# A Fourier and Hyena encoder layer: the first batch's loads and norm rearranged, one token's split done once, products of high parts before those of low parts

## The chip, the cores and the metric

The kernel runs on one core of a Trainium2 chip. Five engines with their own instruction queues work beside each other: TensorE (PE: matmuls, with its weight loads shown apart as PEld), VectorE (DVE), ScalarE (ACT), GpSimd (POOL) and SyncE (SP), which here only issues DMAs. The metric is the device time of the whole program in microseconds.

## What is computed

Two sequences of 1024 tokens and 1024 channels go through one encoder layer in float32. Cut to what matters:

```python
xn = rmsnorm(x, g_pre)
p = xn @ w_in
fv, fg, hv, hg, mg = split(p)                    # 1024, 1024, 3072, 1024, 2048 columns
fz = real(fftn(fv.reshape(B, L, 4, 256), axes=(1, 3), norm="ortho"))
y_f = (fz * silu(fg)) @ w_fourier_out
v, x1, x2 = split(short_conv(hv, w_short))       # width 3 over the sequence
kf = hyena_filters(...)      # small sine network: h = sin(f1*(z@w1+b1)); h = sin(f2*(h@w2+b2)); ...
z = v
for n, gate in enumerate((x1, x2)):
    z = gate * long_conv(z, kf[:, n], hyena_d[n])    # circular convolution of length 2048
y_h = (z * silu(hg)) @ w_hyena_out
g_f, g_h = split(sigmoid(mg + b_merge))
return x + rmsnorm((g_f * y_f + g_h * y_h) @ w_out, g_post)
```

## The kernel before

Every large product is made of three: each float32 operand is split into a high part `h` (rounded to the matmul format `fp32r`) and a low part `l` (the rest), and `mm3` adds `h*h`, `h*l` and `l*h` in one PSUM bank. `split` does it: ScalarE rounds (L171, the rows named CAST), then VectorE or GpSimd subtracts (L181). `mm` (L194) is the line of nearly all matmuls, so in the profile they are told apart by tile names, not by lines.

A planner orders the instructions. The code is traced in program order; the framework simulates a timeline, picks on each engine what is ready with the earlier place in the program first, and writes fixed orders with semaphores. An instruction can move far ahead of its place if its buffer is free. `issue_after(ins)` forces the instructions that a block puts on `ins`'s engine behind `ins`; `keep_in_program_order` pins one. Tiles with the same tag share a given number of buffers.

The stages, in order of time:

- `phase_fourier`, to about 230 us, for batch b = 0 and 1. `hidden(0)` computes the first layer of the sine network: two products (`phd`), a range reduction on VectorE (`sin_of`), two sines on ScalarE with the table that sines need, and a store to `d_h1`. `norm` loads eight row tiles `x` of 128 tokens, squares each on ScalarE with the sum of the row (`ss`), computes the reciprocal root for four rows at a time with three Newton steps in small VectorE instructions (`rstd`, tiles `rs_m`, `rs_t`, `rs`) and scales the identity by it (`dg`). `xtile` then multiplies rows by `dg` for each channel tile k = 0..7, which normalises and transposes at once (`tpx`, two PSUM banks of tag "T", four products of 128 tokens each), copies it out with the gain on ScalarE (`xg`, two buffers, 0.5 MB each), stores it (`d_x`), forms sums and differences of mirrored tokens (`eo`; in batch 1 the difference is made by GpSimd) and splits them (`eh`, `el`). Token 512 has no mirror and is kept apart in `x5`. `weights` loads a tile of `w_fv` (`wfv`), folds it (`wer`, `wor`) and splits it (`we`, `wo`). `pfv` multiplies. In batch 0 and the first half of the channels, six of the eight PSUM results grow while k runs (`begun`: four of the even part, two of the odd part); `fourier_half` makes the other two, splits all eight (`ee`, `oo`), multiplies `x5` (`pfx`), and runs the transforms over tokens with the table `seq` (`pse`, `pso`) and over channels with `chan` (`pP`, `pQ`). Batch 1 and the other halves follow.
- `phase_main`, to about 1700 us: input projections (`inproj`, PSUM `pin`, 1472 products of each of the three kinds), the filters' spectra (`pft`, `pXf`), and the two long convolutions by blocked transforms (`forward`: `pX`; `conv_back`: `pT`). In `inproj` GpSimd makes the low part of the weights (`wl`).
- `phase_gates` (`pg`) and `phase_out` (`pyf`, `pyh` from `project`, `po` from `last_rows`), with a block scheme that takes seven products instead of eight; its products come from `times`.

The tables `seq` (2 MB) and `chan` are loaded by GpSimd's queue, since they change their type on the way. So that they do not start too early, GpSimd first copies one element of `rs`, known only when the norm is done, into them (L531). `alt`, `chx` and `vec` have no such condition.

The lines the prediction touches: 237 to 254 `rstd`, 271 the sines, 317 the row loads, 320 the squares, 325 `dg`, 338 the clearing of two spare columns of `xg`, 344 and 345 the copy to `xg` and its store, 364 the weight load, 173 and 181 the split of `x5`, 531 to 535 the tables, 739 to 742 the weights of `inproj`.

## Time and profile before

| | |
|---|---|
| median of 3 runs | 2446.82 us (2443.44 to 2447.43) |
| profiled execution | 2449.26 us, span of its trace 2447.1 us |
| granted TensorE clock, mean | 0.997 of full speed |
| TensorE busy | 2396.1 us, 13196 matmuls |
| VectorE, ScalarE, GpSimd busy | 1893.8, 1096.8, 485.9 us |
| moved by DMA | 429.36 MB, mean 175 GB/s |

A row of the profile names the line, the engine, the operation and the tiles (`out<-in`), then the shapes, the number of instructions, their busy time and mean length, the idle time of the engine just before them and what ended it. `pin<-xl,wh` is thus a projection with the low part of x and the high part of the weight. Matmuls are pipelined and overlap in the records: those of 512 columns are shown as about 390 ns long and start about 227 ns apart. Small groups are counted by records; a float32 product that is not split shows two. The chain follows the work that ended last backwards to what released each step.

### The profile page before, as it was taken

The numbers are of one execution on the slowest core, as the hardware profiler recorded it, in microseconds if no ns is written. First come the engines' busy times: TensorE is split into PE (matmuls) and PEld (weight loads), VectorE is DVE, ScalarE is ACT, GpSimd is POOL, SyncE is SP. The second block draws the span as 40 slices with busy tenths as digits, with TensorE's granted clock in tenths as the row PEclk, the third lists the DMA queues.
The fourth block names the chain that finished last, engine by engine and source line by source line (L and its number), as shares of the span: only waits on it lengthen the run. The fifth ranks groups of instructions, "written<-read, shape, count | busy, mean of one in ns | idle before, by whom it ended". The sixth has DMA issues, their size and how long they took to land.

```text
span 2447.1 us, 36853 instructions
## 1 busy us (share of the span) xinstructions
PE 2396.1 (98%) x13196; PEld 2082.3 (85%) x13196; DVE 1893.8 (77%) x3405; ACT 1096.8 (45%) x2063; POOL 485.9 (20%) x516
## 2 busy tenths in 40 slices
PE   6999999999999999999999999999999999999998
PEld 5988888888888888888888888888788888888886
DVE  7687888888748999999989999766555455665677
ACT  5545677767633433334223333333344444544343
POOL 1341222222143433331000000112200111122111
PEclk9999999999999999999999999999999999999999
DMA  7545655555555555445434444335454567776543
GB/s 273 170 141 191 224 175 173 167 175 167 173 194 177 172 177 173 165 165 192 146 128 134 141 141 138 121 121 184 154 174 159 198 210 255 245 250 213 169 164 129
DMA packets 225151, 429.36 MB, mean 175 GB/s; under 512 B 23542, under 2 KB 87255, under 8 KB 224456
## 3 DMA queue, kind: packets, MB, share of 16 engines
q1 hardware_dynamic: 198444, 333.34, 41.1%
q0 software_dynamic: 26336, 93.65, 10.9%
q8 instruction: 104, 1.70, 0.3%
q14 instruction: 79, 0.65, 0.1%
q10 hardware_dynamic: 188, 0.02, 0.0%
HBM read 290.60 MB, written 136.31 MB: 174 GB/s over the span
## 4 chain that ended last, share of the span: by engine, by line
PE 88%; DMA 5%; issue 3%; DVE 2%; ACT 1%; POOL 1%; SPq 0%; DVEq 0%; POOLq 0%; ACTq 0%
PE pin L194 41%; PE pT L194 7%; PE pg L194 7%; PE pX L194 7%; PE po L194 6%; PE pyh L194 5%; PE pyf L194 5%; PE pXf L194 3%; PE pfv L194 2%; DMA wr<-in_w_fo 1%; PE pft L194 1%; PE tph L792 1%; DMA wr<-in_w_ho 1%; PE tpx L194 1%; DMA wfv<-in_w_fv 1%
## 5 line engine op out<-in xcount | busy, mean ns | idle before, releaser
L194 PE MATMUL pin<-xh,wl 128*128 128x512 f32 x1472 | 577.2, 392 | 2.6 <-POOL wl L181 2.6
L194 PE MATMUL pin<-xl,wh 128*128 128x512 f32 x1472 | 575.6, 391 | 2.4 <-DVE xl L181 2.4
L194 PE MATMUL pin<-xh,wh 128*128 128x512 f32 x1472 | 576.5, 392 | 0.7 <-DMA wh<-d_w 0.7
L181 POOL TENSOR_TENSOR wl<-wr,wh 128x512 fp32r<-128x512 f32 x136 | 240.3, 1768 | 1144.0 <-ACT wh L171 1105.9
L194 PEld LDWEIGHTS pin<-xh,wl 128*128 128x128 f32 x1472 | 277.1, 188 | 54.9 <-POOL wl L181 4.1
L194 PEld LDWEIGHTS pin<-xl,wh 128*128 128x128 f32 x1472 | 277.1, 188 | 54.3 <-DVE xl L181 3.2
L194 PEld LDWEIGHTS pin<-xh,wh 128*128 128x128 f32 x1472 | 277.1, 188 | 52.1 <-DMA wh<-d_w 1.1
L171 ACT CAST wh<-wr 128x512 fp32r<-128x512 f32 x264 | 162.8, 619 | 346.0 <-PE pin L194 136.8
L194 PE MATMUL pT<-cinv,yh 128*128 128x256 f32 x1024 | 193.1, 283 | 0.0
L194 PEld LDWEIGHTS pT<-cinv,yh 128*128 128x128 f32 x1024 | 164.0, 190 | 9.0
L181 DVE TENSOR_TENSOR t<-pX,k 128x1024 f32<-128x1024 f32 x128 | 155.9, 1218 | 10.9 <-PE pX L194 9.3
L194 PE MATMUL pX<-bh,cfwd 128*128 128x256 f32 x768 | 159.6, 286 | 0.0
L181 DVE TENSOR_TENSOR wl<-wr,wh 128x512 fp32r<-128x512 f32 x128 | 87.2, 687 | 93.5 <-ACT wh L171 93.2
L194 PE MATMUL pyf<-sf,wh 128*128 128x512 f32 x512 | 158.0, 390 | 0.9 <-ACT wh L171 0.9
L194 PE MATMUL pyh<-sh,wh 128*128 128x512 f32 x512 | 157.3, 389 | 0.0
L171 ACT CAST bh<-b 128x512 fp32r<-128x512 f32 x144 | 89.0, 620 | 126.7 <-DVE b L181 84.5
L194 PE MATMUL pT<-cinv,yl 128*128 128x256 f32 x512 | 144.9, 283 | 0.0
L171 ACT CAST yh<-y 128x512 fp32r<-128x512 f32 x128 | 79.2, 619 | 114.1 <-DVE y L181 91.3
L194 PEld LDWEIGHTS pX<-bh,cfwd 128*128 128x128 f32 x768 | 126.3, 190 | 2.5
L194 PEld LDWEIGHTS pyf<-sf,wh 128*128 128x128 f32 x512 | 96.0, 188 | 21.3 <-ACT wh L171 1.6
L194 PEld LDWEIGHTS pyh<-sh,wh 128*128 128x128 f32 x512 | 96.1, 188 | 19.9
L194 PE MATMUL pX<-bl,cfwd 128*128 128x256 f32 x384 | 109.6, 285 | 0.0
(354 smaller groups left out, 5262.7 us busy)
## 6 DMA issues: line engine op xcount, KB each, us to landing
k<-d_k SPq DMA_DIRECT2D x128, 512.0 KB, 4.0
wr<-in_w_in SPq DMA_DIRECT2D x136, 256.0 KB, 3.1
d_g<-gt SPq DMA_DIRECT2D x124, 256.0 KB, 2.6
d_k<-kt SPq DMA_DIRECT2D x128, 128.0 KB, 2.1
d_k<-kt SPq DMA_DIRECT2D x64, 256.0 KB, 2.3
wr<-in_w_fo POOLq DMA_DIRECT2D x64, 256.0 KB, 4.0
g<-d_g SPq DMA_DIRECT2D x64, 256.0 KB, 4.2
wr<-in_w_ho POOLq DMA_DIRECT2D x64, 256.0 KB, 3.7
```

The costliest lines, as they stand in the source:

```text
L171: self.rounded = nc.scalar.copy(h, src)
L181: return e.tensor_tensor(out, a, b, op=op)
L194: return self.nc.tensor.matmul(out, lhsT, rhs, start=start, stop=stop, skip_group_check=shared)
L792: nc.tensor.transpose(tp[:, q * P:(q + 1) * P], eo[:, e, q], self.ident)
```

## The change

- Row loads of batch 0 are issued by SP (even rows) and by ScalarE's queue (odd rows), all before the first square; the load of the first weight tile comes between rows 4 and 6 on SP's queue.
- The norm of batch 0 runs in three groups of rows, 0 to 3, 4 to 6 and 7. The first weight tile is folded before the last group and split behind the last scaling; all other weights' VectorE instructions in that loop are placed behind the last scaling too.
- The two sines of `hidden(0)` and the store behind them come after the last square.
- The tables are asked for when k = 4, and `seq` and `chan` wait for one element of tile 4 (`xg`).
- Token 512 is copied per tile into `r5` by ScalarE and split once after the loop, in both batches.
- In batch 0 the last two results of the odd part start at k = 7, in the two "T" banks, with the products of tiles 0 to 6 ahead of tile 7's.
- In `forward`, `inproj`, `conv_back`, `times` and `project`, the products of the high part of one operand come first and those of its low part last.

```diff
     def rstd(self, pool, out, ss, n):
-        m = pool.tile([P, n], F32, tag=f"rm{n}", name="rs_m", bufs=2)
-        t = pool.tile([P, n], F32, tag=f"rt{n}", name="rs_t", bufs=2)
+        m = pool.tile([P, max(n, 4)], F32, tag="rm", name="rs_m", bufs=2)[:, 0:n]
+        t = pool.tile([P, max(n, 4)], F32, tag="rt", name="rs_t", bufs=2)[:, 0:n]
...
-        nc.scalar.activation(out, y, AF.Sin)
+        return lambda: nc.scalar.activation(out, y, AF.Sin)
...
-            nc.sync.dma_start(x, a[f"x{b}"][m * P:(m + 1) * P, :])
             self.xs.append(x)
+            if b == 0:
+                (nc.scalar if m % 2 else nc.sync).dma_start(x, a[f"x{b}"][m * P:(m + 1) * P, :])
+                if m == 4:
+                    raw = self.weight_rows(pw, 0, 0)
+        lo = 0
+        for m in range(8):
+            x = self.xs[m]
+            if b:
+                nc.sync.dma_start(x, a[f"x{b}"][m * P:(m + 1) * P, :])
             sq = px.tile([P, D], F32, tag="xg", name="sq", bufs=2)
-            nc.scalar.activation(sq, x, AF.Square, accum_out=ss[:, m:m + 1])
-            if m % 4 == 3:
-                q = slice(m - 3, m + 1)
-                self.rstd(px, rs[:, q], ss[:, q], 4)
-                for j in range(m - 3, m + 1):
-                    nc.vector.tensor_scalar(dg[:, j], self.ident, rs[:, j:j + 1], None, op0=MUL)
+            self.squared = nc.scalar.activation(sq, x, AF.Square, accum_out=ss[:, m:m + 1])
+            if m == 7 and b == 0:
+                raw = self.weight_sums(pw, raw, True)
+            if m in ((3, 6, 7), (3, 7))[b]:
+                q = slice(lo, m + 1)
+                self.rstd(px, rs[:, q], ss[:, q], m + 1 - lo)
+                for j in range(lo, m + 1):
+                    self.scaled = nc.vector.tensor_scalar(dg[:, j], self.ident, rs[:, j:j + 1], None, op0=MUL)
+                lo = m + 1
+        if b == 0:
+            with tc.issue_after(self.scaled.ins):
+                self.weight_parts(W, 0, raw, True)
...
-        x5 = fo["x5"][:, k]
-        self.split(x5[:, b:b + 33:32], x5[:, 2 + b:35 + b:32], xg[:, 512:513].to_broadcast([P, 2]), "dve", "dve")
+        nc.scalar.copy(fo["r5"][:, k:k + 1], xg[:, 512:513])
...
+                    end = self.hidden(0, px, pf)
+                if b == 0:
+                    W = self.open_weights(pw)
                 with tc.issue_after(behind.ins) if b else ExitStack():
-                    self.norm(b, px, pf)
+                    self.norm(b, px, pf, pw, W)
+                if b == 0:
+                    with tc.issue_after(self.squared.ins):
+                        end()
...
-                    if b == 0:
-                        self.weights(pw, W, 0, k, True)
+                    if b == 0 and k:
+                        with tc.issue_after(self.scaled.ins):
+                            self.weights(pw, W, 0, k, True)
                     self.xtile(b, k, px, fo)
-                    for (e, m), p in begun.items():
-                        self.pfv(p, e, m, k, W, fo)
-                for half in ((0, 1), (1, 0))[b]:
-                    if b + half == 0:
+                    if (b, k) == (0, 4):
                         nc.sync.dma_start(self.vec, a["c_vec"])
                         for t in ("seq", "chan"):
-                            nc.gpsimd.tensor_copy(fo[t][:, 0, 0:1], self.rs[:, 7:8])
+                            nc.gpsimd.tensor_copy(fo[t][:, 0, 0:1], self.xg[:, 0:1])
...
+                    if (b, k) == (0, 7):
+                        for m in (2, 3):
+                            begun[1, m] = self.psum("T", 2, "pfv1")
+                            for j in range(7):
+                                self.pfv(begun[1, m], 1, m, j, W, fo)
+                    for (e, m), p in begun.items():
+                        self.pfv(p, e, m, k, W, fo)
+                r5 = fo["r5"].unsqueeze(2).to_broadcast([P, 8, 2])
+                self.split(fo["x5"][:, :, b:b + 33:32], fo["x5"][:, :, 2 + b:35 + b:32], r5, "dve", "act")
...
     def inproj(self, sec, mt, b=None):
-            for n in range(2):
-                for kk in range(4):
-                    k = 4 * q + kk
+            for w, xs in ((h, (self.xh, self.xl)), (l, (self.xh,))):
+                for n in range(2):
                     s = slice(512 * n, 512 * n + 512)
-                    self.mm3(ps[:, s], (h[:, kk], l[:, kk]), (self.xh[k][:, s], self.xl[k][:, s]), k == 0, k == 7)
+                    for kk in range(4):
+                        k = 4 * q + kk
+                        for x in xs:
+                            self.mm(ps[:, s], w[:, kk], x[k][:, s], w is h and x is self.xh and k == 0, w is l and k == 7)
...
     def times(self, p, A, B, first):
+        todo = [(0, k, j) for k in range(4) for j in range(2)] + [(1, k, 0) for k in range(4)]
+        for w, k, j in todo:
+            m = self.mm(p, A[w][:, k], B[k][j], first and w + k + j == 0, w + k == 4, True)
```

`weights` is cut into `weight_rows` (load), `weight_sums` (fold) and `weight_parts` (split), with the same instructions. `forward`, `conv_back` and `project` are reordered as `inproj` is.

More of the change, by code (lines that the diff above doesn't have):

```diff
@@ L608, in forward @@
         for i, pr in enumerate(pairs):
-            self.mm3(X[:, i], tab(pr, 0), (h[:, 0:2], l[:, 0:2]), True, False)
-            self.mm3(X[:, i], tab(pr, 1), (h[:, 2:4], l[:, 2:4]), False, True)
+            for d, parts in ((h, (0, 1)), (l, (0,))):
+                for k in range(2):
+                    for t in parts:
+                        self.mm(X[:, i], tab(pr, k)[t], d[:, 2 * k:2 * k + 2], d is h and k + t == 0, d is l and k == 1)
         return X
@@ L1151, in project @@
                     for kk in range(4):
[L1152 to L1153 removed]
+                        for x in S[4 * q + kk]:
+                            self.mm(ps, h[:, kk], x, 4 * q + kk == 0 and x is S[0][0], False)
+                    for kk in range(4):
+                        self.mm(ps, l[:, kk], S[4 * q + kk][0], False, 4 * q + kk == 7)
                 return ps
```

54 lines of the change are left out of this document (31 added, 23 removed).

## The prediction

> **What bounds the kernel now.** I read the page first (busy shares, chain), then TensorE's waits over the whole run, then busy time by stage where those waits lie, and last the order of time of single engines there.
>
> ```profile
> span 2447.1 us, 36853 instructions
> PE 2396.1 (98%) x13196; PEld 2082.3 (85%) x13196; DVE 1893.8 (77%) x3405; ACT 1096.8 (45%) x2063; POOL 485.9 (20%) x516
> PE 88%; DMA 5%; issue 3%; DVE 2%; ACT 1%; POOL 1%; SPq 0%; DVEq 0%; POOLq 0%; ACTq 0%
> ```
>
> TensorE is busy for 2396.1 of 2447.1 us and makes up 88% of the chain. The change takes no product away, so it can win only from the 51 us in which TensorE idles, plus what its clock loses after a pause.
>
> ```profile
> PE tpx L194 <- DMA wfv<-in_w_fv: 9.8, 1, 9.8
> PE tpx L194 <- DVE dg L325: 5.1, 1, 5.1
> PE tpx L194 <- ACT xg L344: 3.5, 2, 2.6
> PE pin L194 <- POOL wl L181: 2.6, 3, 1.4
> PE pin L194 <- DVE xl L181: 2.4, 2, 1.8
> PE pyh L194 <- DVE wl L181: 1.2, 1, 1.2
> ```
>
> Each row has the wait in total, how often and the longest. The first three rows are the start of the first batch (norm factors, normalised tiles). The `wl` rows are waits for the second (low) part of a weight; `xl` is the low part of the other operand.
>
> ```profile
> core 0: us, PE busy (x) PEld busy (x) DVE busy (x) ACT busy (x) POOL busy (x), PEclk, DMA share, GB/s
> 10.00:15.00 5.00, 0.00 (x0) 0.00 (x0) 4.79 (x13) 3.89 (x7) 0.00 (x0) 1.00 1.03 416
> 0.00:25.00 25.00, 6.61 (x15) 3.71 (x16) 16.33 (x59) 14.37 (x25) 3.68 (x15) 1.00 0.79 279
> 25.00:45.00 20.00, 17.20 (x117) 16.73 (x116) 15.92 (x39) 12.39 (x23) 0.77 (x4) 0.91 0.88 304
> 45.00:62.00 17.00, 17.00 (x148) 16.99 (x146) 14.15 (x28) 9.92 (x14) 3.42 (x5) 1.00 0.68 225
> 88.00:100.00 12.00, 9.67 (x69) 9.49 (x68) 7.48 (x35) 8.72 (x20) 0.20 (x2) 0.86 0.77 259
> 120.00:145.00 25.00, 20.80 (x169) 19.59 (x169) 23.34 (x43) 15.10 (x25) 13.02 (x14) 1.00 0.73 252
> 1710.00:1732.00 22.00, 19.53 (x85) 15.54 (x84) 13.24 (x9) 9.76 (x14) 11.44 (x5) 1.00 0.63 225
> 2182.00:2188.00 6.00, 4.82 (x21) 3.63 (x20) 4.63 (x7) 4.13 (x7) 1.07 (x2) 1.00 0.37 129
> ```
>
> Each row is a stretch with the busy time of every engine, the granted clock, the DMA share and the rate. TensorE idles 18.4 us in the first 25, 2.8 in 25 to 45 (with the clock at 0.91, so 20 x 0.09 = 1.8 us more), 2.3 in 88 to 100, 4.2 in 120 to 145, 2.5 around 1710 and 1.2 at 2182. Hence four places: the norm chain, the pause before 38 us, the second batch's tiles, the low weight parts.
>
> **The change part by part.** *Row loads, sines, three norm groups.* ScalarE squares the rows, VectorE makes the factors:
>
> ```profile
> 12.12 1.06 ACT L320 ACTIVATE sq<-x 128x1024 f32<-128x1024 f32 x1 [0.41 <-DMA x<-in_x]
> 14.56 1.28 ACT L271 ACT_TABLE_LOAD   x1
> 15.85 0.63 ACT L271 ACTIVATE hd<-sq 128x512 f32<-128x512 f32 x1
> 17.43 0.61 ACT L271 ACTIVATE hd<-sq 128x512 f32<-128x512 f32 x1
> 18.98 1.04 ACT L320 ACTIVATE sq<-x 128x1024 f32<-128x1024 f32 x1
> ...
> 20.15 0.17 DVE L242 TENSOR_SCALAR rs_m<-ss 128x4 f32<-128x4 f32 x1 [1.52 <-ACT sq L320]
> 23.70 0.16 DVE L253 SCALAR_TENSOR_TENSOR rs<-rs_t,rs 128x4 f32<-128x4 f32 x1
> 23.89 0.88 DVE L325 TENSOR_SCALAR dg<-ident,rs 128x128 f32<-128x128 f32 x4
> ```
>
> Row 3 landed at 12.12, and with 0.524 MB a row at 416 GB/s (1.26 us) row 7 lands near 17.2. Its square starts only at 18.98, because the table load and the two sines take 1.28 + 0.63 + 0.61 = 2.5 us in between. That looks like a gain of 1.8 us. But with two queues rows 6 and 7 arrive together, and the first weight tile (260 KB, 0.63 us) is put ahead of row 6: two squares of 1.25 us (with the read of the sum) from 17.8 end at 20.3, against 20.1 now. If the queues do not pair the rows, the end is near 19.1. So this end moves by -1.0 to +0.2; I take 0, since 1.03 of the DMA engines' time is already in use and a second queue brings no bandwidth.
>
> The DMA page of the Trainium skill (DMA: Bandwidth & Descriptors, section Issuing engines are not separate DMA queues) says that DMAs begun by different engines interleave on the same 16 engines and only the time to issue is saved. By that rule the row loads themselves gain nothing, and the 1.03 row agrees.
>
> The chain behind the last square does get shorter: now 4.1 us from 20.15 to TensorE's start at 24.24 (11 small instructions for four rows, with weight work of VectorE in between, then scalings of 0.2 us). The last group has one row: 9 instructions at 0.2 us (the step from the row at 23.70 to the next at 23.89) and one scaling, 2.1 us; the three-row group runs beside it and the weight work is held behind the last scaling. Gain **2.0 us** (1.8 to 3.0). The sines then hold ScalarE from 20.1 to 22.6; the new factors come at 22.2, and TensorE first has 1.3 us of products for the other PSUM bank of k = 0 (8 of the 40 in 6.85 us below): costed at nothing, 2.5 us if that bank is not free. The sines' store now leaves SP's queue after 22.6, and weight loads behind it wait as long; their users are tiles 1 and 2, some 5 us further on: nothing. The four row issues on ScalarE fall before the first row lands, in time in which ScalarE waits for data: nothing.
>
> *Tables put back.* TensorE's pause before 38.49:
>
> ```profile
> 24.24 6.85 PE L194 MATMUL tpx<-dg,x 128*128 128x128 f32 x40 [5.09 <-DVE dg L325]
> 35.47 0.39 PE L194 MATMUL pfv<-wo,el 128*128 128x256 f32 x2
> 38.49 4.57 PE L194 MATMUL tpx<-dg,x 128*128 128x128 f32 x24 [2.62 <-ACT xg L344]
> ...
> 28.77 8.87 DMA d_x<-xg
> seq<-in_c_seq POOLq DMA_DIRECT2D x1, 2064.0 KB, 8.5
> ```
>
> ScalarE could not write tile 2 because the store of tile 0 (`xg` has two buffers) took 8.87 us against the big table `seq`, which was loading. Idle and lost clock: 2.8 + 1.8 = 4.6 us. The change lets the tables start with tile 4. Tiles 2 and 3 then flow, but the stores of tiles 4 and 5 meet the same 2.1 MB, and tile 6 needs tile 4's buffer. By then TensorE has two tiles of products in hand, so part of the wait is covered. Bounds: 4.6 gained, or 4.0 lost (an 8.87 us wait instead of 4.6); I take half, **2.3 us**. The table would land near 35 + 8.5 = 43.5, ahead of its first use, which follows the batch's last tile. On GpSimd's queue the copies that hold the tables back wait for tile 4, and the clearing of tile 5's two spare columns may queue behind them and the issues; tile 5 is written after tile 4 on ScalarE anyway: nothing. The small tables (`alt`, `chx`) carry no new condition and cost nothing.
>
> *Products of the odd half pulled ahead.* 42 of 48 products of two more banks go ahead of the last tile's: 42 x 17.00/148 = 4.8 us of work, the same in sum. It fills the wait for the last tile and is missing later as cover for the splits and the next weights. The 45 to 62 row shows no idle to fill, so I take 0, at worst minus 4.8.
>
> *Token 512 split once.* Sixteen tiny VectorE instructions per batch go; one 128 x 1 ScalarE copy per tile and two instructions at the end come. In the second batch they are not tiny:
>
> ```profile
> L173 DVE CAST x<-xg 128x2 fp32r<-128x2 f32 x8 | 5.2, 658 | 0.0
> L181 DVE TENSOR_TENSOR x<-xg,x 128x2 fp32r<-128x2 f32 x8 | 2.5, 321 | 0.1
> ...
> 123.49 3.51 POOL L181 TENSOR_TENSOR eo<-xg 128x512 f32<-128x512 f32 x2 [0.91 <-ACT xg L344]
> 124.06 1.48 DVE L173 CAST x<-xg 128x2 fp32r<-128x2 f32 x1
> 125.57 1.45 DVE L181 TENSOR_TENSOR x<-xg,x 128x2 fp32r<-128x2 f32 x1
> ```
>
> In 120 to 145 VectorE is busy 23.34 of 25 us and TensorE idles 4.2. Two elements take 1.48 us while GpSimd's subtractions run, so the 7.7 us (5.2 + 2.5, from 112 to 148) are mostly waiting for GpSimd. Upper bound 4.2 us, lower 0: the next VectorE instruction may inherit the wait. I take **1.5 us**. ScalarE has 15.10 of 25 us in use, so eight copies hide there.
>
> The SBUF page of the Trainium skill (SBUF — State Buffer, section Who interferes with whom) says that VectorE and GpSimd share a port pair as an exclusive lock, which also an instruction with two SBUF inputs must take. The trace agrees (the cast ends 0.03 us after GpSimd's first instruction). By that rule the lock passes to the next subtraction and this term is 0 instead of 1.5, the sum 2438.5.
>
> *High parts first.* In `inproj`, `project`, `times`, `forward` and `conv_back` the low part is needed later, in `inproj` by 16 matmuls, 16 x 19.53/85 = 3.7 us. The waits for `wl` (2.6 and 1.2, longest 1.4) are shorter than that and go, with a few tenths elsewhere: **4.0 us**. The waits for `xl` (2.4) stay, since it is still needed second. Bounds 0 to 5. Late next would be the high part.
>
> Sum: 2.0 + 2.3 + 1.5 + 4.0 = 9.8 us. The profiled execution took 2449.26 us (span 2447.1 and 2.2 around it), which gives 2439.5; the median of the runs is 2.4 lower, 2446.82, so the forecast for it is **2437.0**.
>
> **The rivals.** *A, the collisions dissolve.* The stores miss the tables altogether (4.6 instead of 2.3) and the second batch's idle goes (4.2 instead of 1.5): 2432.0. If the 2.3 us idle and the slow clock (12 x 0.14 = 1.7) of 88 to 100 also go because everything there arrives at another moment, 2428.0. For it: DMA had free time before 24 us. Against: the tables have to load somewhere.
>
> *B, the front parts do nothing.* The rows land as late as bandwidth lets them, the pause moves from tile 2 to tile 6, the lock of GpSimd passes to the next subtraction, and the used-up cover costs 2: only 4.0 - 2.0 remain, 2444.8. The lock rule of the SBUF page above is the reason for the third of these.
>
> *C, the planner spends the slack.* The order on each engine comes from a planned timeline. With the low parts due 3.7 us later, it can put their splits later among other work of GpSimd and VectorE.
>
> ```profile
> L181 POOL TENSOR_TENSOR wl<-wr,wh 128x512 fp32r<-128x512 f32 x136 | 240.3, 1768 | 1144.0 <-ACT wh L171 1105.9
> ```
>
> GpSimd splits 136 pieces at 1.77 us on average, which vary with the lock. Each late split costs some 1.3 us (2.6 for 3, longest 1.4). Four such cancel the 4.0; at (9.8 + 4.9)/1.3 = 11 of the 136 the kernel is slower by 0.2%; with 12, 2452. For it: GpSimd's idle time before these splits (1144 us) leaves a planner much room. Against: only three are late now.
>
> **How the numbers follow.** 0.2% (4.9 us) is about what a measurement of this kernel can tell from no change. Forecast 0.54 (its own range 2431 to 2442), A 0.16, B 0.17, C 0.13. Faster: nearly all of the forecast, A, and a bit of B: 0.70. Same: most of B and the forecast's upper end: 0.17. Slower: C, 0.13. The range goes from a little below A's far end to half way between B and C: 2426 to 2449.
>
> **What would show it.** Right: first products of the second half of rows near 22.2 instead of 24.24; no pause at 36 to 38, and a shorter one near 43; waits for `wl` gone from TensorE's list; 120 to 145's stretch with less than 4.2 us idle. Wrong: last square later than 20.5; the 8.87 us store again, now at tile 4, with a pause as long; waits of `pin` for `wl` in more places than three; TensorE idle right after the last tile of the first batch, where the pulled products are missing.

## The result, and the profile after

The changed kernel takes 2456.44 us (median of six runs, 2451.47 to 2458.39); the kernel before took 2446.32 us beside it (six runs, 2443.44 to 2450.08). The ratio is 1.0042 (95% interval 1.0032 to 1.0053): slower by 0.4%, against a forecast of 2437.0 us, and above the range's end of 2449. The profiled execution took 2456.95 us, with a span of 2455.2 us against 2447.1. The kernel before was profiled in an execution of 2449.26 us, some 3 us above its median, so single stages below carry an uncertainty of a few us.

The page of the changed kernel, first lines and chain:

```profile
span 2455.2 us, 36926 instructions
PE 2399.0 (98%) x13196; PEld 2081.4 (85%) x13196; DVE 1908.8 (78%) x3384; ACT 1102.0 (45%) x2081; POOL 496.1 (20%) x516
PE 46%; DVE 6%; issue 5%; DMA 3%; POOL 1%; ACT 1%; SPq 0%; DVEq 0%; POOLq 0%; ACTq 0%
```

TensorE does the same 13196 products, but its share of the chain falls from 88% to 46%. The two are not to be compared as they stand: the shares after add up to 62% only, because the chain, followed back from the end, breaks off at 936.8 us. What can be read is that just behind that point it runs through VectorE's instructions and not through TensorE's. VectorE is busy 15.0 us longer with 21 instructions fewer.

The quickest way to see where time went is to follow one product per stage. The rows are those of single tiles on TensorE: count, duration, then the first and the last start in the window looked at. The last start is what counts here. Before:

```profile
L194 PE MATMUL pfv<-wo,el x24: 280/284/286, 195.1 to 205.7; 128*128 128x256 f32 x24
L194 PE MATMUL pQ<-px,chx x2: 280/282/283, 252.2 to 259.1; 128*128 128x258 f32 x1, 128*128 128x256 f32 x1
L194 PE MATMUL pin<-xh,wl x11: 389/389/389, 1735.0 to 1741.8; 128*128 128x512 f32 x11
L194 PE MATMUL pg<-th,a2l x4: 389/389/389, 1933.7 to 1935.8; 128*128 128x512 f32 x4
L194 PE MATMUL pyf<-sf,wl x9: 389/389/389, 2235.7 to 2241.2; 128*128 128x512 f32 x9
L194 PE MATMUL po<-bh,mxh x8: 388/389/389, 2434.5 to 2437.0; 128*128 128x512 f32 x8
```

After:

```profile
L194 PE MATMUL pfv<-wo,el x12: 278/281/285, 195.0 to 200.1; 128*128 128x256 f32 x12
L194 PE MATMUL pQ<-px,chx x2: 283/284/284, 250.7 to 257.4; 128*128 128x258 f32 x1, 128*128 128x256 f32 x1
L194 PE MATMUL pin<-xh,wl x16: 389/389/389, 1737.5 to 1744.5; 128*128 128x512 f32 x16
L194 PE MATMUL pg<-th,a2l x4: 389/389/389, 1937.4 to 1938.1; 128*128 128x512 f32 x4
L194 PE MATMUL pyf<-sf,wl x20: 389/389/389, 2237.3 to 2248.9; 128*128 128x512 f32 x20
L194 PE MATMUL po<-bh,mxh x8: 388/389/389, 2442.2 to 2444.7; 128*128 128x512 f32 x8
```

At 200 us the changed kernel is 5.6 us ahead (205.7 - 200.1). At the last `pQ` 1.7 are left, and even that flatters it, for the planner puts nine fewer products of the next stage ahead of that row (1644 precede it instead of 1653). Counting products shows more. The first 231 us, before and after (columns: length, busy time and number of instructions of TensorE, its weight loads, VectorE, ScalarE, GpSimd, then clock, DMA share, GB/s):

```profile
0.00:231.00 231.00, 197.09 (x1504) 186.45 (x1505) 173.12 (x422) 126.55 (x251) 60.00 (x86) 0.99 0.57 196
0.00:231.00 231.00, 197.00 (x1501) 183.76 (x1502) 171.22 (x402) 129.86 (x270) 67.43 (x86) 0.99 0.58 196
```

With 1504 products begun against 1501, nothing of the lead is left 31 us later. The 1500th product starts at 230.7 us instead of 230.4, so the main stage then loses some 2.4 us (from 0.3 to 2.7 behind; that is net of 2.5 us of waits for `wl` that are gone), the gates nothing, the output stage 5.4, and the rest nothing. The front did what was forecast in sum up to 200 us; three other places took it back and more.

TensorE's waits in the changed kernel, over the whole run (total, times, longest):

```profile
PE pQ L194 <- DVE fB L177: 6.8, 1, 6.8
PE pyf L194 <- ACT wh L171: 5.5, 3, 3.2
PE pT L194 <- DVE yl L181: 1.8, 2, 1.6
PE tpx L194 <- ACT xg L364: 1.1, 4, 0.3
PE pT L194 <- ACT T1s L889: 1.0, 1, 1.0
PE pT L194 <- ACT yh L171: 0.9, 2, 0.6
PE pyh L194 <- DVE wl L181: 0.4, 1, 0.4
```

These are seven of its 19 rows. Two of the same rows before:

```profile
PE pQ L194 <- DVE fB L177: 2.0, 1, 2.0
PE pyf L194 <- ACT wh L171: 0.9, 1, 0.9
```

`pin` waits for `wl` no more (2.6 us before), `pyh` for 0.4 us (1.2). The waits of `pQ` for `fB` and of `pyf` for the high part `wh` have grown, from 2.0 to 6.8 and from 0.9 to 5.5 us. New is `pT`, which waits for VectorE's and ScalarE's work. The stretches that the prediction read, after the change (same columns):

```profile
10.00:15.00 5.00, 0.00 (x0) 0.00 (x0) 3.60 (x9) 4.35 (x9) 0.00 (x0) 1.00 1.07 408
25.00:45.00 20.00, 19.03 (x160) 18.39 (x158) 19.34 (x40) 16.22 (x35) 8.04 (x4) 1.00 0.73 252
45.00:62.00 17.00, 16.09 (x135) 15.80 (x134) 10.13 (x15) 7.22 (x14) 3.94 (x9) 1.00 0.84 300
120.00:145.00 25.00, 21.92 (x177) 21.07 (x178) 23.91 (x35) 16.36 (x35) 10.28 (x9) 1.00 0.53 180
1710.00:1732.00 22.00, 22.00 (x99) 18.22 (x98) 13.56 (x12) 8.25 (x10) 6.41 (x4) 1.00 0.57 191
```

TensorE idles 1.0 us in 25 to 45 (2.8 before) at full clock (0.91), 0.9 in 45 to 62 (0), 3.1 in 120 to 145 (4.2), and 0 around 1710 (2.5).

### The profile page after: what moved, and what is told of

The parts are those of the page before. It is cut to its first block, busy times and chain, and to the rows that moved or that the text cites. A ratio compares the mean times of both kernels' runs of the same rounds, so it can differ in the third digit from the quotient of the medians.

```text
span 2455.2 us, 36926 instructions
## 1 busy us (share of the span) xinstructions
PE 2399.0 (98%) x13196; PEld 2081.4 (85%) x13196; DVE 1908.8 (78%) x3384; ACT 1102.0 (45%) x2081; POOL 496.1 (20%) x516
## 3 DMA queue, kind: packets, MB, share of 16 engines
q0 software_dynamic: 26336, 93.65, 11.1%
## 4 chain that ended last, share of the span: by engine, by line
PE 46%; DVE 6%; issue 5%; DMA 3%; POOL 1%; ACT 1%; SPq 0%; DVEq 0%; POOLq 0%; ACTq 0%
PE pin L194 17%; PE pg L194 7%; PE po L194 6%; PE pT L194 5%; PE pyh L194 4%; PE pX L194 4%; PE pyf L194 2%; DMA wr<-in_w_fo 1%; DVE b L181 1%; DMA g<-d_g 1%; POOL wr L1189 1%; DVE x L177 1%; DVE t L181 1%; PE tph L839 1%; DVE yl L181 0%
## 5 line engine op out<-in xcount | busy, mean ns | idle before, releaser
L194 PE MATMUL pin<-xh,wl 128*128 128x512 f32 x1472 | 382.6, 391 | 0.0
L194 PEld LDWEIGHTS pin<-xh,wl 128*128 128x128 f32 x1472 | 270.2, 188 | 51.0
L194 PE MATMUL pT<-cinv,yh 128*128 128x256 f32 x1024 | 165.0, 283 | 2.1 <-ACT T1s L889 1.0
L194 PEld LDWEIGHTS pT<-cinv,yh 128*128 128x128 f32 x1024 | 145.3, 190 | 9.9 <-ACT yh L171 2.5
L194 PE MATMUL pyf<-sf,wh 128*128 128x512 f32 x512 | 128.4, 394 | 5.6 <-ACT wh L171 5.5
L194 PE MATMUL pX<-bh,cfwd 128*128 128x256 f32 x768 | 131.0, 287 | 0.0
L194 PE MATMUL pyh<-sh,wh 128*128 128x512 f32 x512 | 126.5, 389 | 0.0
L194 PEld LDWEIGHTS pX<-bh,cfwd 128*128 128x128 f32 x768 | 110.3, 190 | 3.9
L181 DVE TENSOR_TENSOR bl<-b,bh 128x512 fp32r<-128x512 f32 x144 | 104.8, 730 | 7.1 <-ACT bh L171 6.9
L194 PE MATMUL pT<-cinv,yl 128*128 128x256 f32 x512 | 104.1, 285 | 1.8 <-DVE yl L181 1.8
```

The costliest lines, as they stand in the source:

```text
L181: return e.tensor_tensor(out, a, b, op=op)
L194: return self.nc.tensor.matmul(out, lhsT, rhs, start=start, stop=stop, skip_group_check=shared)
```

## The experiments

All kernels are compared with the kernel before on the same chip. Theory O says that the new orders of products cost the time, each at its place; theory P says that the planner writes other fixed orders whenever anything moves, so that stalls come and go with no edit to blame. "Last `pfv`" and "last `pQ`" are starts as above; "main" is from the last `pQ` to the last `pin`, "output" from the last `pg` to the last `pyf`, all read from the same rows; "VectorE" is its busy time in the 220 us from 900 to 1120. The ratio comes from 4 to 10 executions of a kernel, each of the other columns from a single one. The last `pQ` has 1644 to 1653 products ahead of it, so it and "main" are to be read to about 2 us. "Excess" in the expectations is the time by which a stretch runs behind an even spacing of its products: TensorE's idle time and what its clock loses.

| run | kernel | ratio (95%) | last `pfv` | last `pQ` | VectorE | main | output |
|---|---|---|---|---|---|---|---|
| | before | 1 | 205.7 | 259.1 | 212.4 | 1482.7 | 305.4 |
| | changed | 1.0042 (1.0032, 1.0053) | 200.1 | 257.4 | 219.3 | 1487.1 | 310.8 |
| e1 | changed, all orders old | 1.0024 (1.0014, 1.0034) | 199.1 | 255.5 | 212.4 | 1487.3 | 305.2 |
| e2 | before, all orders new | 1.0050 (1.0034, 1.0067) | 203.7 | 256.2 | 219.3 | 1484.8 | 305.5 |
| e4 | changed, `inproj` old | 1.0010 (1.0001, 1.0020) | 199.1 | 255.8 | 213.5 | 1481.5 | 305.9 |
| e6 | before, `inproj` new | 1.0004 (0.9994, 1.0015) | 202.3 | 254.9 | 217.3 | 1482.9 | 304.7 |
| e13 | before, `inproj`, `forward`, `conv_back` new | 1.0025 (1.0016, 1.0035) | 205.0 | 257.9 | 219.3 | 1486.3 | 303.9 |
| e7 | changed, gate product cut | 1.0006 (0.9996, 1.0015) | 199.7 | 256.7 | 213.5 | 1477.9 | 308.3 |
| e8 | changed, `inproj`, `project` old | 1.0002 (0.9992, 1.0011) | 198.4 | 255.0 | 214.6 | 1482.1 | 310.1 |
| e9 | e8, `times` old too | 1.0003 (0.9993, 1.0012) | 200.7 | 257.2 | 214.6 | 1484.1 | 305.3 |
| e14 | changed, `times` old | 1.0037 (1.0026, 1.0048) | 201.3 | 258.7 | 219.3 | 1486.3 | 302.8 |
| e3 | changed, `hid` held back | 1.0057 (1.0042, 1.0072) | 198.9 | 257.9 | 219.3 | 1487.5 | 311.6 |
| e5 | e4, next stage held back | 1.0009 (1.0000, 1.0019) | 201.5 | 257.7 | 214.6 | 1481.1 | 310.0 |
| e10 | e9, held back, `fB` by SyncE | 0.9999 (0.9990, 1.0009) | 199.4 | 254.3 | 211.8 | 1483.6 | 302.3 |
| e11 | before, token 512 alone | 0.9993 (0.9983, 1.0002) | 200.8 | 254.2 | 212.2 | 1483.4 | 304.3 |
| e12 | before, `fB` by SyncE | 1.0028 (1.0018, 1.0037) | 204.9 | 260.6 | 212.4 | 1486.6 | 301.9 |
| e15 | e10, `project` new | 1.0007 (0.9998, 1.0017) | 199.6 | 254.7 | 212.8 | 1484.6 | 302.0 |

**Front or orders: e1 and e2.** e1 undoes all five orders in the changed kernel, e2 makes them alone in the kernel before. In `inproj`, e1:

```diff
-            for w, xs in ((h, (self.xh, self.xl)), (l, (self.xh,))):
...
+            for n in range(2):
+                for kk in range(4):
...
+                    self.mm3(ps[:, s], (h[:, kk], l[:, kk]), (self.xh[k][:, s], self.xl[k][:, s]), k == 0, k == 7)
```

> The changed kernel with the old order of products (high*high, high*low, low*high one after the other) in forward, inproj, conv_back, times and project; everything that the change did to the first batch stays. Theory O (the new orders lose the time, in the convolutions and in the output stage; the front gained its 5 us): the excess over an even spacing of the products stays near 24 us in the first 100 us, and vanishes from 955 to 1102 (6.5 us now) and shrinks at 2125 to 2220 (5 us now); 2440 to 2444 us. Theory P (the fixed orders that the planner writes come out differently whenever anything moves, and the losses are not tied to one edit): the front keeps its gain, but stalls of the same size turn up at other places, or the same ones stay; 2444 to 2456 us. The stall of 6.9 us at 202.7 stays by a theory that puts it down to the front's shift, and goes by one that puts it down to the new orders.

> The kernel before with the new order of products alone (high part of one operand first, low part last) in forward, inproj, conv_back, times and project. Theory O: the front is as before (29 us of excess in the first 100 us), and the losses of 955 to 1102 (6.5 us) and 2125 to 2220 (5 us) are there, less the 2.9 us of waits for low weight parts that go: 2454 to 2456 us. The prediction's term taken alone would be 4.0 us of gain, 2443 us. Theory P: waits for low weight parts gone, and stalls elsewhere that no one edit explains: 2446 to 2456 us.

e2 took 2455.3 us, which lies in the ranges of both theories and far from the 2443 of the prediction's term. VectorE's 219.3 us and the stalls of 955 to 1102 come with the orders (TensorE idles 3.3 us from 900 to 1120, 0 before), as theory O says. The loss near 2125 to 2220 that it expected too is hardly there: the output stage takes 305.5 us against 305.4. e1 lost the stalls (TensorE idles 0 us from 900 to 1120) but was 0.24% slower than before, not faster. Its last `pfv` is 6.6 us earlier, but its 1800th product, near 287 us, only 0.6 us, and TensorE idles 3.6 us between 235 and 900 (0.2 in the kernel before). So the front's gain is lost on the way without any new order, and theory P is right in part. The whole 0.24% is not found in the traces: the medians differ by 6.0 us, the spans of the two profiled executions by 1.0.

**The main stage: e4, e6, e13, e7.** e4 takes back `inproj` alone, e6 makes it alone, e13 makes it with both convolution orders; for `inproj` the diff is the one above. e7 leaves GpSimd with two columns of each gate product and cuts the rest of that product:

```diff
-                    self.mul("pool", X[i][:, s], X[i][:, s], sg[q])
+                    if q:
+                        self.mul("pool", X[i][:, 0:2], X[i][:, 0:2], sg[0][:, 0:2])
+                        self.mul("pool", X[i][:, 512:514], X[i][:, 512:514], sg[1][:, 0:2])
```

> The changed kernel with the old order of products in inproj alone. If the loss of 955 to 1102 comes from inproj's new order (GpSimd's splits of weights fall on VectorE's butterfly instructions, which then take 813 ns instead of 413), VectorE's busy time in 900 to 1100 goes from 199.6 back to about 192.5 us and the 6.5 us of stalls go, while the 2.9 us of waits for low weight parts near 1710 come back: 2452 us. If it comes from the orders in forward and conv_back, VectorE stays full there and the time goes up by the 2.9 us: 2459 us.

> The kernel before with the new order of products in inproj alone. Theory I (inproj's order causes the stalls of 955 to 1102): they are there at the same places (6 us), VectorE's busy time of 900 to 1120 is 219 instead of 212 us, and nothing is lost at 2210; 2449 to 2453 us. Theory P (any edit shifts the fixed orders and the stalls fall by chance): the stalls are elsewhere or missing; 2441 to 2455 us.

> The kernel before with the new order of products in inproj, forward and conv_back. If inproj's order and that of the convolutions together make VectorE full in 900 to 1120, its busy time is 219 us there and the excess of 955 to 1102 is 5 to 7 us, as with all five (e2_order), and the pause near 2210 is under 1.2 us, since times is old: ratio 1.001 to 1.004. If the other two orders are needed as well, the excess is about 2 us as with inproj alone: ratio 0.999 to 1.001.

> The changed kernel with GpSimd's products of the gate (x<-x,sg, 512 columns each) cut to two columns each; the gate's product is left out, so the output is another. Theory G (VectorE fills up in 900 to 1120 because GpSimd's instructions coincide with its small sums b<-xt,bs): VectorE's busy time there falls from 219 to 212 us or less, and most of the 6 us of waits for yl, yh and T1s go; 2449 to 2451 us. Rival: VectorE is full there because of its own order and of work moved into this stretch; busy time stays over 217 us and the waits stay; 2455 us or more.

The order in `inproj` alone fills VectorE half way (217.3), with the orders in the convolutions wholly (219.3 in e2, e13, e14, e3 and the changed kernel); without it, VectorE never passes 214.6. e6 was a miss for theory I in the time, and e13 showed that it takes both: TensorE idles 4.7 us from 900 to 1120 there, 0.6 in e6, and 0 in e4, e8 and e9, which have the convolutions' new orders without `inproj`'s. e4 was 6 us faster than its 2452 us: the waits of `pin` for `wl` did not come back, and its output stage was 4.9 us shorter without any edit there. The whole stretch from 900 to 1120 before, in the changed kernel and in e7 (columns as in the prediction's stretches):

```profile
900.00:1120.00 220.00, 220.00 (x1334) 196.33 (x1333) 212.35 (x335) 83.66 (x151) 76.54 (x72) 1.00 0.50 166
```

```profile
900.00:1120.00 220.00, 215.66 (x1296) 190.16 (x1296) 219.29 (x325) 80.05 (x144) 74.42 (x70) 1.00 0.51 159
```

```profile
900.00:1120.00 220.00, 220.00 (x1332) 196.38 (x1331) 213.53 (x333) 85.90 (x152) 69.73 (x71) 1.00 0.50 166
```

Busy groups in it tell what happens (count, busy time, mean ns, idle before and its releaser). Of the kernel before:

```profile
L181 DVE TENSOR_TENSOR b<-xt,bs 128x256 f32<-128x256 f32 x16 | 6.9, 467 | 0.0
L181 POOL TENSOR_TENSOR wl<-wr,wh 128x512 fp32r<-128x512 f32 x24 | 42.6, 1774 | 142.7 <-ACT wh L171 142.7
```

Changed:

```profile
L181 DVE TENSOR_TENSOR b<-xt,bs 128x256 f32<-128x256 f32 x14 | 10.9, 813 | 0.0
L181 POOL TENSOR_TENSOR wl<-wr,wh 128x512 fp32r<-128x512 f32 x23 | 41.4, 1801 | 47.2 <-PE pin L194 36.0 <-issue 11.1
```

e7:

```profile
L181 DVE TENSOR_TENSOR b<-xt,bs 128x256 f32<-128x256 f32 x16 | 6.5, 444 | 0.5 <-ACT bs L622 0.5
```

GpSimd's split of the low part used to start as soon as ScalarE had rounded the high part. Now the high part is used up before the low part, its buffer is free earlier, the rounding runs ahead, and the split then waits for TensorE to free the low part's buffer (36.0 us for 23). GpSimd's work so falls on other instructions of VectorE: the small sums `b<-xt,bs` take 813 ns instead of 467. The trace shows the coincidence one by one: in the changed kernel nine of the 14 sums have no product or subtraction of GpSimd beside them and take 410 ns on average; the other five overlap with its gate products or its splits and take 1234 to 1918 ns. With 219.3 of 220 us VectorE has no slack left, and TensorE idles 4.3 us (220 - 215.66), mostly waiting for `yl`, `yh` and `T1s`. e7 agrees: the split still waits for TensorE (65.7 us for 24), but with the gate products cut the sums take 444 ns, VectorE 213.5 us, and TensorE idles 0 us in the stretch. It was better than forecast, 2445.8 us.

**The output stage: e8, e9, e14.** e8 takes back `inproj` and `project`, e9 `times` too, e14 `times` alone:

```diff
-        todo = [(0, k, j) for k in range(4) for j in range(2)] + [(1, k, 0) for k in range(4)]
-        for w, k, j in todo:
...
+        for k in range(4):
+            h, l = A[0][:, k], A[1][:, k]
+            for j, (w, x) in enumerate(((h, B[k][0]), (h, B[k][1]), (l, B[k][0]))):
```

> The changed kernel with the old order of products in inproj and in project; forward, conv_back and times keep the new one. If project's order makes the pause of 3.0 us before 2208 (the high part of the next weight is late, because ScalarE's queue stands behind a gate that is still loading), that pause shrinks to 1 us or less, and a wait for a low weight part of about 1 us comes back near 2185: 2443 to 2445 us. If the pause comes from how the stage falls in time, it stays at 2 to 3.5 us: 2446 us.

> The changed kernel with the old order of products in inproj, project and times; forward and conv_back keep the new one. In all kernels so far with the new order in times, forward and conv_back, SyncE issues eight loads of sh ahead of the load of g near 2205, ScalarE waits 7 us for g with the weight casts behind it, and TensorE pauses 2.3 to 4.3 us and loses 1.7 to 3.4 us of clock; in the kernels without, the pause is 0.5 to 1.0 us. If the order in times causes it, the pause near 2205 falls to 1 us or less: ratio to the kernel before 0.997 to 0.999. If forward and conv_back cause it, the pause stays at 2 us or more: ratio 1.000 to 1.002.

> The changed kernel with the old order of products in times alone. If times alone carries the loss of 2100 to 2290, the excess there falls from 8.5 to 4 us or less, no time at half clock near 2220, while the stalls of 200 to 225 (12.8 with the clock) and of 955 to 1102 (6.5) stay: ratio 1.001 to 1.003. If it does not, the pauses of 1.7 us near 2126 and 3.4 near 2217 stay: ratio 1.004.

`project`'s order is not the cause (e8 still takes 310.1 us for the stage). The order in `times` goes with the loss in all kernels: in the seven that have it new TensorE waits 2.1 to 5.7 us for `wh` from 2100 to 2290 and the stage takes 305.5 to 311.6 us, in the ten that have it old 0 to 1.0 and 301.9 to 305.4. What it costs the whole program is not shown: e9 came out at 1.0003 beside e8's 1.0002, and not below 0.999. Waits from 2100 to 2290, in the changed kernel:

```profile
ACT g L1221 <- DMA g<-d_g: 35.4, 14, 6.9
PE pyf L194 <- ACT wh L171: 5.5, 3, 3.2
```

and in e14:

```profile
ACT g L1222 <- DMA g<-d_g: 25.6, 11, 5.6
PE pyf L194 <- ACT wh L171: 1.0, 1, 1.0
```

ScalarE works in a fixed order, and the roundings of the next weights stand behind the sigmoid of a gate that is still loading; when the gate is 1 us later, the roundings are late and TensorE stops. But `times` has no product between the last `pg` and the last `pyf`. Its order can act there only through the order that the planner writes for loads and ScalarE; the expectation that SyncE's eight loads of `sh` ahead of `g` are the reason did not hold, since e14 has them too. How the one leads to the other stays open. e14 as a whole cannot be told from the changed kernel (1.0037 against 1.0042, with intervals that overlap), though its output stage is 8.0 us shorter in the profiled executions: other stages of it were longer.

**The stage boundary: e3, e5, e10.** In the changed kernel VectorE, 202 to 209 (start, duration, and in brackets the idle time before and its releaser):

```profile
202.83 0.48 DVE L177 SCALAR_TENSOR_TENSOR fA<-pQ,vec,fPs 128x258 f32<-128x258 f32 x1 [1.56 <-PE pQ L194]
207.28 1.22 DVE L181 TENSOR_TENSOR hid<-hidr,hid 64x1024 fp32r<-64x1024 f32 x1 [3.97 <-ACT hid L929]
208.52 0.43 DVE L181 TENSOR_TENSOR fB<-pQ,fPm 128x258 f32<-128x258 f32 x1
```

A subtraction of the next stage stands ahead of `fB` and waits for its own load and rounding. That load had moved with the lead (issued at 200.3 us instead of 205.9, landed at 206.2 instead of 210.8); what changed is the subtraction's place. It goes with the front: in all seven kernels with the new front and nothing held back the subtraction stands ahead of this `fB` and `pQ` waits 6.0 to 6.8 us, in the kernel before, e2, e6 and e13 it stands behind and `pQ` waits 2.0 to 2.1. In the kernel before the subtraction came later, and only the store of `fB` was waited for:

```profile
209.43 0.43 DVE L181 TENSOR_TENSOR fB<-pQ,fPm 128x258 f32<-128x258 f32 x1 [0.95 <-DMA d_fz<-fB]
...
213.42 1.22 DVE L181 TENSOR_TENSOR hid<-hidr,hid 64x1024 fp32r<-64x1024 f32 x1
```

e3 forces that subtraction behind the last instruction of the half (first part below), e5 (on e4) all first work of the next stage, on ScalarE too; e10 (on e9) does as e5 and also moves a store (second part):

```diff
-            self.sub("dve", self.hid[64:128], hid[64:128], self.hid[64:128])
+            with tc.issue_after(self.half_done.ins):
+                self.sub("dve", self.hid[64:128], hid[64:128], self.hid[64:128])
...
-            nc.gpsimd.dma_start(self.d_fz[b][2 * gg + 1], B[:, 0:1024])
+            nc.sync.dma_start(self.d_fz[b][2 * gg + 1], B[:, 0:1024])
```

> The changed kernel with one instruction held back: the subtraction that makes the low part of hid is put behind the last VectorE instruction that mixes pP and pQ of the second batch's first half. If the stall at 202.7 comes from that subtraction standing ahead of fB in VectorE's order while its own data are late (a load that lands at 206.21 and a cast until 207.25), fB comes at about 204 to 205 instead of 208.5, the 6.9 us stall shrinks to 3 or less and the 6.8 us at half clock behind it goes: 4 to 8 us less, 2448 to 2452 us. If fB waited for its buffer's store instead, fB stays at 208 or later and the time is the same, 2456 us. By theory P the later stages may move by some us either way, and only 200 to 225 us is to be read.

> The changed kernel with the old order in inproj (2446.2 us as measured) and, besides, the first work of the next stage (the casts and the subtraction of hid, the first decay rates and taps) held back on VectorE and on ScalarE behind the last mixing of pP and pQ of the second batch's first half. Holding back the subtraction alone brought fB from 208.5 to 204.2, but a second wait of 2.9 us came 5 us later. If that second wait came from the next stage's ScalarE work (cast of hid, table load, exponentials) standing ahead of fPm, both waits go: the excess of 200 to 235 falls from 12 to 5 to 8 us, 2440 to 2443 us. If the stores of fA and fB limit the stage (they share the DMA engines with eight loads of 0.5 MB), the same stall of 4 us or more stays at the next fA or fB, and the time is 2445 us or more.

> The kernel of the run e9_fc with the next stage's first work held back on VectorE and ScalarE (as in e5_bound), and with the store of fB issued by SyncE instead of GpSimd (where it stands behind the store of fA). fB has one buffer, and its next use waits for its store: 4.7 to 5.4 us from issue to landing. If that store is what gives back the front's gain, it lands in 3.5 us or less, the pause near 202 shrinks from 6.2 (3.7 in e5_bound) to 2 us or less, no time at half clock follows, and the last pQ comes at 252 to 254 instead of 255 to 258: ratio 0.994 to 0.998. If the DMA engines are simply full there, the store takes as long and the loads of the next stage come later: last pQ at 255 or later, ratio as for e9_fc.

e3, VectorE:

```profile
204.21 0.43 DVE L181 TENSOR_TENSOR fB<-pQ,fPm 128x258 f32<-128x258 f32 x1 [2.13 <-DMA d_fz<-fB]
...
209.71 0.43 DVE L181 TENSOR_TENSOR fB<-pQ,fPm 128x255 f32<-128x255 f32 x1 [2.06 <-ACT fPm L501]
```

e10, VectorE:

```profile
203.09 0.49 DVE L177 SCALAR_TENSOR_TENSOR fA<-pQ,vec,fPs 128x258 f32<-128x258 f32 x1 [2.50 <-DMA d_fz<-fA]
```

In e3 `fB` came at 204.21, as expected, but 5 us later `fPm` was late in the same way behind the next stage's exponentials on ScalarE, and the last `pQ` did not move (257.9). With both held back (e5) the store remained (3.5 us of waiting), the last `pQ` was at 257.7, and the 2440 to 2443 us expected were 2447.1. In e10 the wait is 2.50 us for the store of `fA`, and the last `pQ` is at 254.3, near the 252 to 254 expected; the ratio of 0.994 to 0.998 was not reached. Over all runs: in the eleven kernels with the new front the last `pfv` starts at 198.4 to 201.5 and the last `pQ` at 254.3 to 258.7 (mean 256.4); in the five with the old front (without e11) at 202.3 to 205.7 and 254.9 to 260.6 (mean 257.7). Of 4.5 us of lead (mean of `pfv` 199.8 against 204.3) 1.3 arrive. Counted by products it is plainer: the 1800th starts at 287.0 us on average with the old front and at 287.1 in the nine kernels with the new one that do not have both of e10's edits, so nothing arrives; in e10 and e15, which have both, it starts at 282.8 and 283.2. (With 282.5 e11, old front but for token 512, comes as early, so a difference of 4 us here need not have this cause.) Each cover that is taken away shows the next wait: the next stage's instructions on VectorE, then on ScalarE, then the stores.

**One part alone, one edit that should mean nothing, and all together: e11, e12, e15.** e11 makes the change to token 512 alone; e12 only gives `fB`'s store to SyncE in the kernel before (the second part of the diff above); e15 is e10 with `project`'s new order.

> The kernel before with one part of the change: token 512 is copied by ScalarE for each tile and split once behind the loop. The prediction's term is 1.5 us (0 to 4.2) in the stretch from 112 to 148, where TensorE idles 4.2 us of 36. If the 5.2 and 2.5 us of tiny VectorE instructions held the tiles up, the idle falls to 2.7 us or less. If VectorE's next instruction inherits the wait for GpSimd, its own instructions get longer by as much and the idle stays near 4.2. The time of the whole may differ by some us through other fixed orders; only 112 to 148 is to be read.

> The kernel before with one edit: the store of fB is issued by SyncE instead of GpSimd. There TensorE waits 2.2 us for fB near 208, and fB for its buffer's store. If the place behind fA's store on GpSimd's queue is what makes the store late, that wait falls to 1.5 us or less and the last pQ comes 1 us earlier (before: 259.1, and 255 to 256 in other kernels with the old front): ratio 0.999. If other loads take the bandwidth, nothing changes there: ratio 1.000. It also shows how much the time moves when one DMA is given to another queue and all else is as before.

> The changed kernel without the three losses as far as they are known: inproj and times in the old order, the next stage's first work held back and fB stored by SyncE. forward, conv_back and project keep the new order, the front all of the change. By the prediction's sum without inproj's and times' share: the front's 5 us, 4 us of the 5 to 6 at the stage boundary, and the waits for wl near 2185: excess of 0 to 200 near 29, of 200 to 235 near 8.6, last pQ near 254, 2437 to 2441 us, ratio 0.997 to 0.999. By theory P other stalls turn up (in 300 to 500, 1130 to 1150 or near 1715, where they come and go between kernels by up to 6 us): ratio 0.999 to 1.001.

The stretch from 112 to 148, before:

```profile
112.00:148.00 36.00, 31.80 (x264) 30.45 (x264) 32.41 (x59) 22.75 (x37) 17.00 (x16) 1.00 0.67 228
```

and in e11:

```profile
112.00:148.00 36.00, 33.15 (x273) 31.67 (x272) 31.88 (x50) 22.86 (x46) 15.32 (x15) 1.00 0.61 216
```

e11's idle falls from 4.2 to 2.85 us, close to the 2.7 expected. It has the best median beside the kernel before (2443.31 against 2444.62), though its interval still holds 1. e12 moves one DMA to another queue. The wait for `fB` that it was to shorten stays (2.5 us, 2.0 before), and the kernel gets 0.28% slower, with its main stage 3.9 us longer. From 165 us on TensorE has its products in another order, so this much can come from a new set of fixed orders that nobody meant. e10 and e15 keep the front's gain past the last `pQ` and lack the losses of `inproj` and `times`, and are still no faster than before in the median. Both wait for `wl` again between 1700 and 1725 (TensorE idles 1.9 us in e10 and 4.0 in e15 from 1690 to 1760, none in e9), but that does not explain it: their profiled executions are 6.7 and 4.6 us shorter in span than that of the kernel before, which lies 4.6 and 4.7 us above the medians that they were measured against. Where the gain goes in the median is not shown. No version beat the kernel before beyond the interval.

## Why the prediction was wrong

*Norm chain: right in the sum, not in its parts.* First products of the second half of rows, changed kernel:

```profile
21.54 0.80 PE L194 MATMUL tpx<-dg,x 128*128 128x128 f32 x2 [0.94 <-DVE dg L341]
```

21.54 instead of 24.24: 2.7 us, forecast 2.0 (1.8 to 3.0). These are rows 4 to 6; TensorE's idle time in the first 25 us falls by 2.5 (18.39 to 15.90). The last square, and the last row's scaling:

```profile
18.33 1.04 ACT L334 ACTIVATE sq<-x 128x1024 f32<-128x1024 f32 x1
22.43 0.29 DVE L341 TENSOR_SCALAR dg<-ident,rs 128x128 f32<-128x128 f32 x1
```

The square and the read of its sum are over at 19.5, 0.6 us earlier than 20.1, within the forecast's -1.0 to +0.2. From there the last row's scaling ends 3.2 us later (22.72) and not the 2.1 of the forecast, as the small instructions of the two groups take turns on VectorE. The earlier square made up for half of that, which is luck. The rows arrive at 408 GB/s against 416. Here the rule of the Trainium skill (DMA: Bandwidth & Descriptors, section Issuing engines are not separate DMA queues) and the trace agree: a second queue brought no bandwidth.

*Tables: the number right, the way not.* Forecast 2.3; idle and lost clock in 25 to 45 fall by 1.8 + 1.8, and 0.9 us of idle is new in 45 to 62: 2.7 us. But the tables did not start with tile 4. The copy of one element that holds them back, 0.18 us long before, is now

```profile
37.26 8.49 POOL L563 CAST seq<-xg 128x1 fp32r<-128x1 f32 x1 [1.92 <-ACT xg L364]
```

and 8.48 to 8.50 us in all eleven kernels with the new front. So `seq` was asked for at 46.05 us and landed at 56.05, not near 43.5. The slow stores are there, 10.4 and 10.1 us long, but they are those of tiles 6 and 7, for whose buffers no tile of the batch waits any more. That the collision fell behind the last tile was luck. The copies, which the prediction put at nothing, held tile 4's buffer: ScalarE waited 2.15 us for them, and behind it TensorE the 0.9 us.

*Token 512: right.* Forecast 1.5; 1.1 in the changed kernel, 1.35 alone (33.15 - 31.80). From 112 to 148 TensorE idles 4.0 to 4.2 us in all five kernels with the old split and 2.2 to 3.1 in the twelve with the new. The rival by the rule of the Trainium skill (SBUF — State Buffer, section Who interferes with whom), that the lock passes to the next instruction and nothing is won, is half right: instructions worth 7.7 us went, but VectorE's busy time in e11 fell only from 32.41 to 31.88. Others did inherit part of the wait (`el` 1.6 us longer, `pp` 1.3, the copy `xx` 1.4), and more work fell into the stretch (273 products against 264); TensorE gained all the same.

*High parts first: the step that failed.* The term was a gain of 4.0 us; the orders alone (e2) cost 11.1 (2455.3 against 2444.2). The waits for `wl` went as forecast here (2.5 us around 1710, 0.8 of `pyh`), the first of them by luck: in the six other kernels with the new order in `inproj`, `pin` has no such wait either, but `pg` of the next stage waits 1.1 to 2.6 us for its own `wl`. What failed is its bounds "0 to 5": a loss was left out, because the order was judged only by when the low part is needed. It also decides when a buffer comes free, and so when GpSimd runs beside VectorE, which had 212.4 of 220 us in use: 4.3 us of TensorE's time. And `times`, priced with the others at a gain, goes with the 5.4 us of the output stage. Rival C named the planner but priced late low splits; TensorE's waits list shows none of `pin`. Its chance of 0.13 was for the wrong mechanism. In its other sign, "late next would be the high part" was written without a price; `pyf` waiting 5.5 us for `wh` is that price.

*The sum: failed too.* It added gains at 20 to 150 us to the end, 5.8 of its 9.8 us; the front alone (e1) made the kernel 6.0 us slower. The steps between were not asked whether they would follow. At 200 to 210 the planner had put a subtraction that waits for a load ahead of `fB`, `pQ` waited 6.8 us instead of 2.0, and of the lead of 5.6 us nothing was left at 231. Odd-half products pulled ahead were costed at 0 (worst -4.8); TensorE's idle time from 62 to 88 rose from 0.2 to 1.7 us (26.00 - 25.79 and 26.00 - 24.32), and 1.1 us of it is `pfv` waiting for `we`, the next weights, where the used-up cover would be missed. In all eleven kernels with the new front it is 1.7 to 1.8 us, in the six others 0.1 to 0.9. That part was not undone alone, so its share stays open.

## What to carry to other kernels

A gain early in a kernel counts only as far as the next place where a store, a load or another stage's instruction sets the time: look for that place before adding it to the end. When products are put in another order, list not only who needs what later but which buffer comes free earlier, whose work that pulls forward, and what it then runs beside. With orders written by a planner, measure an edit that should mean nothing (here 0.28%) before an effect of that size is put down to an edit that means something.

## What the runs showed of the hardware

In TensorE's pause for `fB` in the changed kernel the granted clock fell to half, and it stayed low into the work behind the pause. Two stretches, inside and after it (clock in the third column from the end):

```profile
206.50:209.80 3.30, 0.01 (x1) 0.01 (x1) 2.50 (x5) 3.27 (x6) 0.00 (x0) 0.50 0.24 79
209.80:213.50 3.70, 3.70 (x19) 3.23 (x20) 1.86 (x5) 1.45 (x4) 0.53 (x2) 0.59 0.40 101
```

So this 6.8 us wait cost about 1.5 us more (3.7 x 0.41), which no list of waits shows.

The GpSimd copy of 8.49 us falls into a stretch that VectorE fills without a gap (busy 8.40 of the 8.40 us from 37.30 to 45.70). The same copy took 0.18 us in the kernels with the old front. That VectorE's work holds it up was not tested alone.

And profiled executions of one kernel stray: e2's took 2450.14 us with a median of 2455.3, which is more than most effects looked for here. Readings that hold in every kernel with an edit and in none without it are therefore safer than single pairs.
